# Hybrid decoder block on one core: the gates' first factors made once in the first chunk, kept in DRAM, and the head of the gates' stage reordered

## The chip, the cores and the metric

The kernel runs on one core of one Trainium2 chip. The metric is the device time in microseconds of that core. The core has a matrix engine (PE, with its weight loads shown as PEld), a vector engine (DVE), a scalar engine (ACT), a general engine (POOL), a queue engine (SP) and 16 DMA engines. SP issues nearly all DMAs; POOL issues those that add to their destination.

## What is computed

One decoder layer on x of 2048 tokens by 1024 channels, all in float32:

```python
h = rmsnorm(x, attn_norm)
z = h @ w_in                      # pool channels | q | k | v | gate_pool | gate_attn
g_pool, g_attn = split(sigmoid(z[..., o4:] + b_gate))
a = pool_mixer(u_pool, w_pool, pool_scale)     # windows 2, 4, 8, 16; per-group linear map
b = swa_sink_attention(q, k, v, sinks)         # window 128, QK-norm, partial rotary
x = x + (g_pool * a + g_attn * b) @ w_out
h = rmsnorm(x, ffn_norm)
up = causal_depthwise_conv(h @ w_up, conv_w, conv_b)
x = x + (silu(gate) * val) @ w_down
```

The change touches the gates: the two products of h with the 1024 gate columns each.

## The kernel before, in words

**Precision.** PE multiplies rounded float32 (`F32R`). Each operand is kept as a high part (ACT rounds it) and a low part (DVE takes the difference), and a product is three matmuls: high x high, high x low, low x high.

**Stages.** The sequence is cut into two chunks of 1024 tokens (`T`), so all stages run twice. In a chunk, `mixer` makes keys, values and queries, then attention, then calls `gates`; `out_proj`, `up` and `Down` follow. Attention is 32 items: four groups of four heads, in the order `q4` = 3, 2, 1, 0, each with eight blocks of 128 queries. Between two items stand matmuls that fill PE, the `fillers` of that group: projections of queries (`q`), pool channels (`pu`) and the gates of channel slabs 6 and 7 (`ga`, `pg`). In the last group (number 3) the last two items' fillers are the first products of the gates' stage, `one` and `two` of units 0 and 1.

**The gates' stage.** It computes the gates of the other six slabs, one `Gates` unit each (`u0` to `u5`). A unit multiplies a 2 x 2 block matrix (k halves by the two gates) with a 2 x 2 block input (k halves by token halves) in seven block products in place of eight: `one` to `seven`, and `early` for the product with `B22` where it is issued before its sum. So it needs sums of weight blocks and sums of input blocks, each split in high and low parts. The weight side is made by `Blocks` (line 326) from two raw slabs of 512 KB in four steps: `first` gives A11 and A12, `second` gives A22, `third` gives S3 and S2, `fourth` gives S1 and S4. A whole-size step is an ACT pass (L348) and a DVE pass (L349) over 128 x 1024, done by `halved`; `second` and the sums use half-size operations (L364 to L377). With `early` the last two steps change places. The input side is made from `xT`: `load_input` (L1386) loads a tile of 128 x 2 x 1024, `scale_input` (L1394) multiplies it by the norm's gain on ACT (L1397), and `right_t1` to `right_t4` (L1122 to L1154) make the sums T1 to T4 and split them by `parted` (L1032, L1033).

**What sets the order.** Weights come by a `Stream`: `get` hands out the next entry of `weight_order`, asks for raw tiles two entries ahead, and splits the next ones. A pair for the gates has the key `("gates", i)`. The order on each engine follows the program, but an instruction may be put earlier where its inputs and buffers are there and the engine is free; `issue_after` forbids it for single ones. Each engine then runs its own list strictly in order, and SP and POOL do so with their DMAs: one that waits holds all behind it. Buffers are pools of tagged slots: `U` has 19 (8 KB a partition), `R`, for raw weights, 3, `M` 5, `F` 4, `Q` 6. In PSUM the scores have one bank pair, `s`, which all exponentials of an item (L880) must have read before the next scores (L861).

**Kept weights.** The second chunk reads made weights back: `keep_weights` stores some, and for the two first pairs of the up-projection `Blocks.store` writes all four parts to DRAM tiles and `Kept.fetch` loads them by name (`PARTS`).

Of the kernel before, what the change touches and what calls it, by code (L numbers as in the profile page):

```python
# [16 lines left out]
F32 = mybir.dt.float32  # L17
F32R = mybir.dt.float32r
I32 = mybir.dt.int32
U8 = mybir.dt.uint8  # L20
AF = mybir.ActivationFunctionType
ALU = mybir.AluOpType
# [4 lines left out]
P = 128  # L27
# [112 lines left out]
def fillers(c, i):  # L140

    q = queries_of(0) + queries_of(1)
    g = gates_of(0)
    pu = [pooled_of(j) for j in range(4)]
    if i == 3:
        out = [[f] for f in g[6:] + pu[3]]
        out[3].insert(0, ("gates", 0, 0))
        out[5].insert(0, ("gates", 1, 0))
        return out + [[("one", i, 0), ("two", i, 0)] for i in range(2)]
    fold = [("fold", j, 0) for j in FOLDS[FOLD_FIRST:] if c == 0 and i == 0]  # L150
    out = fold + (q[:4] + pu[0][2:] + q[4:6], q[6:] + pu[1][:2] + g[:2] + pu[1][2:],
                  pu[2][:2] + g[2:6] + pu[2][2:])[i]
    return [out[n * len(out) // NB:(n + 1) * len(out) // NB] for n in range(NB)]


# [50 lines left out]
def block_kernel(ctx: ExitStack, tc: tile.TileContext, x, xT, pos, vec, qkn, w_poolT, w_pool, w_q, w_kv,  # L206
# [9 lines left out]
    up_ = pool("up", 19)  # L216
# [8 lines left out]
    def load(dst, src):  # L225
        nc.sync.dma_start(dst, src)

    def split(hi, lo, src):
        n = src.shape[1] // 2
        for i in range(2):  # L230
            t = slice(i * n, (i + 1) * n)
            high = A.copy(hi[:, t], src[:, t])  # L232
            low = V.tensor_sub(lo[:, t], src[:, t], hi[:, t].bitcast(F32))  # L233
        return high.ins, low.ins

    def halves(h, t, src, gain):

# [69 lines left out]
    class Kept:  # L307


        def __init__(self, f):  # L310
            self.f, self.w = f, {}
# [15 lines left out]
    class Blocks:  # L327
# [3 lines left out]

        def __init__(self, raws, early=False):
            self.raws, self.w, self.at = raws, {}, 0
            self.steps = [self.first, self.second] + [self.third, self.fourth][::-1 if early else 1]
            self.tiles = []

        def store(self, f):
            kept[f] = []  # L340
            for i, t in enumerate(self.tiles):
                kept[f].append(dp.tile(list(t.shape), F32, f"kept_{f}_{i}"))
                load(kept[f][-1], t.bitcast(F32))

        def halved(self, first, second, raw):
            t = up_.tile([P, 2, 8, P], F32R, "U")
            self.tiles.append(t)
            A.copy(t[:, 0], raw)  # L348
            V.tensor_sub(t[:, 1], raw, t[:, 0].bitcast(F32))  # L349
            self.w[first], self.w[second] = t[:, :, 0:4], t[:, :, 4:8]  # L350

        def step(self, n=1):
            for _ in range(n):
                if self.at < 4:
                    self.steps[self.at]()
                    self.at += 1

        def first(self):
# [65 lines left out]
    class Input:  # L424
# [8 lines left out]
        def pair(self, j, n):  # L433
            return self.t[j, n]

        def fresh(self, k):
            if k % 2 == 0:
                for n in range(2):
                    self.t[k // 2, n] = up_.tile([P, 2, 2, 512], F32R, "U")

    def make_h(c, n, hs, ks=range(KT)):

        a, b = ((0, 256), (256, 512), (512, T))[n] if c == 0 else (0, T)
        for k in ks:
            gain = vc[:, V_AN + k:V_AN + k + 1]
            if n == 0:
                hs.fresh(k)
            if c == 0:
                halves(hs.at(k, n // 2), slice(a % 512, a % 512 + b - a), xs0[k // 2][:, k % 2, a:b], gain)
            else:  # L450
                src = mp.tile([P, T], F32, "M")
                load(src, xT[k * P:(k + 1) * P, c * T:(c + 1) * T])
                for i in range(2):
                    halves(hs.at(k, i), slice(0, 512), src[:, 512 * i:512 * i + 512], gain)
# [562 lines left out]
    def filler(kind, j, n, *a):  # L1017
        if kind == "fold":
            fold(j)
        elif kind == "gates":  # L1020
            a[-1]["units"][j].w = stream.get("gates", j)
        elif kind in ("one", "two"):
            getattr(a[-1]["units"][j], kind)()
        else:
            {"ga": gate_attn, "pu": pooled, "pg": gated, "q": queries}[kind](a[0], j, n, *a[1:])
# [93 lines left out]
        normed(xg[j], 0, pb)  # L1119
        b.setdefault("B11" if j < 2 else "B21", []).append(parted(xg[j][:, :, N0]))  # L1120

    def right_t1(xg, b, pb):  # L1122
        for j in range(2):
            normed(xg[j], 1, pb)
            q11, q12 = xg[j][:, :, N0], xg[j][:, :, N1]
            V.tensor_sub(q11, q12, q11)
            b.setdefault("T1", []).append(parted(q11))
# [259 lines left out]
    def load_input(c, j):  # L1387

        t = up_.tile([P, 2, T], F32, "U")
        load(t, xT[2 * j * P:(2 * j + 2) * P, c * T:(c + 1) * T]  # L1390
             .rearrange("(k p) t -> p k t", p=P))
        return t
# [7 lines left out]
    def gates(c, units, b, xg, last_probabilities, last_values):  # L1400


        def weights(f, n):
            if f < len(units):
                if units[f].w is None:
                    units[f].w = stream.get("gates", f)
                units[f].w.step(n)

        u0, u1, u2 = units[:3]
        xg += [load_input(c, j) for j in (2, 3)]  # L1410
        weights(2, 1)
        u2.one("t")
        last_probabilities()
        weights(1, 2)
        u2.two()
        last_values()
        u0.four()
        u0.early()
        for j in (2, 3):
            scale_input(xg[j], j)  # L1420
        t2s = right_t2(xg, b, None)
        u1.four("a")
        u1.early()
        right_t3(xg, b)
        u0.three()
        u0.six()
        weights(1, 1)
        u0.five()
        right_t4(xg, b, t2s)
        u0.fetch()  # L1430
        u1.three()
        u1.six()
        u0.attn()
        u0.seven()
        u0.value()
        weights(2, 1)
        u1.five()
        u0.combine()
        weights(2, 2)
        n = len(units)  # L1440
        for f in range(2, n):
            u, old = units[f], units[f - 1]
            if f > 2:
                u.one()
                u.two()
            old.fetch()
            old.attn()
            weights(f + 1, 1)
            if f == n - 1:
                mixes = {j: mixed(j) for j in (3, 2, 1)}  # L1450
            old.seven()
            old.value()
            weights(f + 1, 1)
            u.three()
            u.four()
            old.combine()
            if f == n - 1:
                ms = {j: [parted(mixes[j][:, :, N0])] for j in (3, 2, 1)}
                x0 = up_.tile([P, 2, 2, 512], F32R, "U")
                old.parts(x0)  # L1460
                stream.part(stream.used + 2)
            weights(f + 1, 1)
            u.five()
            u.early()
            u.six()
            weights(f + 1, 1)
        u.fetch()
        u.attn()
        u.value(N1)
        u.seven()  # L1470
        u.value(N0)
        for c_ in (N0, N1):
            u.combine(c_)
            if c_ == N0:
                u.parts(x0)
        ms[0] = [x0]
        return ms, mixes
# [144 lines left out]
    def mixer(c, hs, kvw):  # L1622
# [49 lines left out]
        for i in range(len(items)):  # L1672
            group, n = divmod(i, NB)
            chain = scores(items[i])
            if i + 2 < len(items):
                load_queries(items[i + 2])
            if i > 1:
                values(items[i - 2])
            run_later(0)
            fills = fillers(c, group)[n]  # L1680
            last = chain
            for j, f in enumerate(fills):
                if i > 0 and j == (len(fills) > 1):
                    last = probabilities(items[i - 1], chain)
                if j == (len(fills) > 1):
                    run_later(2, last)
                filler(*f, c, hs, ta, st)
            if group == 3:
                if 3 <= n < 7:
                    units[0].w.step(1)  # L1690
                if n == 5:
                    run_later(9)
                    units[1].w.step(1)
                    xg.append(load_input(c, 0))
                if n == 6:
                    scale_input(xg[0], 0)
                    xg.append(load_input(c, 1))
                if n == 7:
                    scale_input(xg[1], 1)
        values(items[-2])  # L1700
        run_later(9)
        right_t1(xg, b, None)
        return gates(c, units, b, xg, lambda: probabilities(items[-1]), lambda: values(items[-1]))

    high, low = split_weights.last
# [103 lines left out]
```

## Time and profile before

| | us |
|---|---|
| median of 3 runs | 2420.15 (2419.64 to 2424.95) |
| the profiled run | 2421.1 |
| its span, first to last instruction | 2419.2 |
| groups 1 and 2 of attention, first chunk | about 195 to 315 |
| group 3, first chunk | about 315 to 376 |
| joint of attention and gates' stage, first chunk | 365 to 420 |
| the same joint, second chunk | 1557 to 1612 |

How to read the profile. The page gives the busy time of each engine, and its share of the span. The table by stage gives, for a stretch of time, the busy time of each engine with the number of instructions, the granted clock of PE (1.00 is full), the share in which the 16 DMA engines were busy, and the rate. A row of the timeline gives start, duration, engine, line, operation, the tile written and the tiles read, the shapes, how many instructions were merged, and in brackets how long the engine had been idle before and what it waited for. A row of the groups gives the busy time and mean ns, then the idle time before. A row of DMA issues ends with the number, the size of one and the median time from issue to landing.

### The profile page before, as it was taken

How to read it: one execution, taken by the hardware profiler on the slowest of the kernel's cores; microseconds unless marked ns; L12 is line 12 of the kernel's file. 1: busy time of each engine (PE TensorE's matmuls, PEld its weight loads, DVE VectorE, ACT ScalarE, POOL GpSimd, SP SyncE). 2: the span in 40 equal slices, each digit the busy share in tenths (PEclk: the TensorE clock that was granted, in tenths of full speed). 3: DMA queues.
4: the chain of work that ended last, by engine and by line, in shares of the span. 5: the costliest groups of instructions: out<-in, count | busy, mean ns of one | idle time of the engine just before them, and what ended most of it. 6: DMA issues, size and time to landing. Idle time of an engine off the chain costs nothing.

```text
span 2419.2 us, 30260 instructions
## 1 busy us (share of the span) xinstructions
PE 2376.2 (98%) x11108; PEld 1971.5 (81%) x11108; DVE 1906.2 (79%) x2934; ACT 1187.9 (49%) x2179; POOL 178.4 (7%) x118
## 2 busy tenths in 40 slices
PE   8999998999999999999999999999999999999999
PEld 7888886877888888788888888778888888888887
DVE  8678888876977777799946867898578777779994
ACT  6545446454555555543622544464546545454432
POOL 0114221000000000000002232200000000000000
PEclk9999999999999999999999999999999999999999
DMA  9568765688222333545244675546742222228421
GB/s 358 203 191 245 222 179 170 212 278 308 90 79 82 101 115 105 190 175 165 96 154 138 185 210 169 161 140 222 226 170 90 93 88 79 79 70 287 140 70 52
DMA packets 160404, 386.08 MB, mean 160 GB/s; under 512 B 13952, under 2 KB 50304, under 8 KB 152320
## 3 DMA queue, kind: packets, MB, share of 16 engines
q1 hardware_dynamic: 155472, 375.58, 46.5%
q0 software_dynamic: 4352, 8.39, 2.2%
q8 instruction: 87, 1.43, 0.2%
q14 instruction: 61, 0.50, 0.1%
q10 hardware_dynamic: 432, 0.19, 0.0%
HBM read 258.93 MB, written 125.17 MB: 159 GB/s over the span
## 4 chain that ended last, share of the span: by engine, by line
PE 88%; DVE 4%; DMA 3%; ACT 3%; issue 1%; POOL 0%; SPq 0%; DVEq 0%; ACTq 0%
PE f L1159 22%; PE f L249 22%; PE t L1159 13%; PE a L1159 6%; PE f L1603 4%; PE a L1603 4%; PE s L1603 4%; PE t L1603 4%; PE a L922 2%; PE s L861 2%; PE a L249 1%; PE t L894 1%; DMA U<-xT 1%; DMA tad<-U 1%; ACT Q L880 0%
## 5 line engine op out<-in xcount | busy, mean ns | idle before, releaser
L249 PE MATMUL f<-U,U 128*128 128x512 f32 (+1 forms) x2784 | 649.2, 389 | 7.5 <-ACT U L232 3.4
L249 PEld LDWEIGHTS f<-U,U 128*128 128x128 f32 x2784 | 510.2, 188 | 113.4 <-DVE U L233 4.9
L1159 PE MATMUL f<-U,U 128*128 128x512 f32 x1872 | 450.1, 391 | 4.5 <-ACT Q L1177 4.5
L1159 PEld LDWEIGHTS f<-U,U 128*128 128x128 f32 x1872 | 352.6, 189 | 80.0 <-ACT Q L1177 6.2
L1225 DVE SCALAR_TENSOR_TENSOR M<-F,vc,M 128x1024 f32<-128x1024 f32 x176 | 225.2, 1281 | 140.8 <-ACT M L1222 140.5
L1159 PE MATMUL t<-U,U 128*128 128x512 f32 x1392 | 330.0, 391 | 6.1 <-ACT U L348 3.6
L1159 PEld LDWEIGHTS t<-U,U 128*128 128x128 f32 x1392 | 262.0, 189 | 62.5 <-ACT U L348 4.4
L348 ACT CAST U<-R 128x1024 fp32r<-128x1024 f32 x156 | 163.1, 1053 | 72.3 <-DVE R L377 37.4
L349 DVE TENSOR_TENSOR U<-R,U 128x1024 fp32r<-128x1024 f32 x156 | 190.7, 1226 | 2.7 <-ACT U L348 2.7
L1159 PE MATMUL a<-U,U 128*128 128x512 f32 x768 | 187.3, 391 | 0.0
L1159 PEld LDWEIGHTS a<-U,U 128*128 128x128 f32 x768 | 143.5, 188 | 29.9 <-ACT Q L1177 0.4
L1159 PE MATMUL f<-U,M 128*128 128x512 f32 x624 | 150.7, 389 | 0.3 <-DVE F L1203 0.3
L880 ACT ACTIVATE Q<-s,st,rq 128x128 f32<-128x128 f32 x256 | 113.8, 456 | 53.1 <-DVE st L877 52.7
L1159 PEld LDWEIGHTS f<-U,M 128*128 128x128 f32 x624 | 117.1, 188 | 25.0 <-DVE F L1203 0.8
L902 POOL TENSOR_SCALAR_AFFINE_SELECT M<-M 128x1024 fp32r<-128x1024 f32 x64 | 97.4, 1522 | 372.5 <-DVE st L882 246.0
L1211 ACT COPY F<-f 128x512 f32<-128x512 f32 x52 | 30.5, 586 | 186.2 <-PE f L1159 186.2
L1561 ACT CAST U<-U 128x1024 fp32r<-128x1024 f32 x76 | 79.0, 1051 | 83.6 <-PE s L1603 21.6
L1222 ACT ACTIVATE M<-F,vc 128x1024 f32<-128x1024 f32 x88 | 109.4, 1243 | 2.0 <-DVE F L1207 0.5
L929 ACT COPY U<-a 128x512 f32<-128x512 f32 x64 | 37.6, 588 | 117.5 <-PE a L922 117.3
L1562 DVE TENSOR_TENSOR U<-U,U 128x1024 fp32r<-128x1024 f32 x76 | 91.9, 1218 | 3.3 <-ACT U L1561 3.1
L1561 ACT CAST F<-U 128x1024 fp32r<-128x1024 f32 x44 | 46.1, 1049 | 93.5 <-PE a L1603 63.8
L1177 ACT COPY Q<-f 128x512 f32<-128x512 f32 x104 | 60.8, 585 | 60.7 <-PE f L1159 60.6
(280 smaller groups left out, 3747.8 us busy)
## 6 DMA issues: line engine op xcount, KB each, us to landing
R<-w_up SPq DMA_DIRECT2D x80, 512.0 KB, 3.8
actd<-M SPq DMA_DIRECT2D x44, 512.0 KB, 2.7
U<-w_down SPq DMA_DIRECT2D x88, 256.0 KB, 5.2
U<-actd SPq DMA_DIRECT2D x88, 256.0 KB, 5.3
qd<-U SPq DMA_DIRECT2D x64, 256.0 KB, 3.8
Q<-qd SPq DMA_DIRECT2D x64, 256.0 KB, 4.7
R<-w_out SPq DMA_DIRECT2D x32, 512.0 KB, 5.2
U<-kept SPq DMA_DIRECT2D x12, 1024.0 KB, 6.7
```

The lines of the kernel that those rows point to most:

```text
L249: nc.tensor.matmul(out, a, b, start=(i == 0), stop=(i == n - 1))
L348: A.copy(t[:, 0], raw)
L349: V.tensor_sub(t[:, 1], raw, t[:, 0].bitcast(F32))
L880: A.activation(pr[:, h, :], sc[:, h, 0:P], AF.Exp, bias=nm[:, h:h + 1], scale=it["rq"][:, h:h + 1], accum_out=rs[:, h:h + 1])
L902: G.affine_select(own.rearrange("p a h q -> p (a h) q"), pa.bitcast(F32).rearrange("p a h q -> p (a h) q"), pattern=[[0, 8], [1, P]], base ...
L1159: nc.tensor.matmul(bank, a[:, x, k, :], b[k // 2][:, y, k % 2, :], start=(first and i == 0), stop=(i == 11), skip_group_check=True)
L1177: Up.last = A.copy(t, bank).ins
L1222: A.activation(y, u[:, 2:], AF.Identity, bias=cw[:, 3, m:m + 1], scale=cw[:, 2, m:m + 1])
L1225: V.scalar_tensor_tensor(y, u[:, j:j + T], cw[:, j, m:m + 1], y, op0=ALU.mult, op1=ALU.add)
L1561: A.copy(hi, src)
L1562: V.tensor_sub(lo, src, hi.bitcast(F32))
L1603: nc.tensor.matmul(into[m], u[:, 0, c_], v[:, 1], start=(first and j == 0), stop=(k == n - 1 and j == 2), skip_group_check=True)
```

## The change

The pairs `gates` 0 and 1 leave group 3. In the first chunk they are taken at the start of groups 1 and 2, and after every second item one step is made and stored to DRAM at once (`step(1)`, `store`). For these two pairs `halved` no longer subtracts on DVE: ACT writes the high part and the negated input, and a DMA from POOL adds the input to the latter (`split_added`). In both chunks group 3 and the gates' stage then fetch the parts by `Kept`. `Blocks` always makes its steps in the order 1, 2, 3, 4. The first step of unit 2 moves from the stage into group 3, the loads of `xT` tiles 0 and 1 and the first half of `right_t1` move one item or more forward, the loads of tiles 2 and 3 stand behind `last_values`, and the rest of the stage's head is reordered. At the start of the first chunk, a one-element memset on POOL takes the four input tiles of the second token half as soon as the others are taken.

```diff
 def fillers(c, i):
...
     if i == 3:
         out = [[f] for f in g[6:] + pu[3]]
-        out[3].insert(0, ("gates", 0, 0))
-        out[5].insert(0, ("gates", 1, 0))
         return out + [[("one", i, 0), ("two", i, 0)] for i in range(2)]
...
+    if c == 0 and i in (1, 2):
+        out = [[f] for f in out]
+        out[0].insert(0, ("gates", i - 1, 0))
+        return out
...
+    def split_added(hi, lo, src):
+
+        A.copy(hi, src)
+        A.activation(lo, src, AF.Copy, scale=-1.0)
+        G.dma_start(lo, src.bitcast(F32R), accum_op=ALU.add)
...
-        def __init__(self, raws, early=False):
-            self.raws, self.w, self.at = raws, {}, 0
-            self.steps = [self.first, self.second] + [self.third, self.fourth][::-1 if early else 1]
+        def __init__(self, raws, added=False):
+            self.raws, self.w, self.at, self.added = raws, {}, 0, added
             self.tiles = []
 
         def store(self, f):
-            kept[f] = []
-            for i, t in enumerate(self.tiles):
-                kept[f].append(dp.tile(list(t.shape), F32, f"kept_{f}_{i}"))
-                load(kept[f][-1], t.bitcast(F32))
+            done = kept.setdefault(f, [])
+            for i in range(len(done), len(self.tiles)):
+                t = self.tiles[i]
+                done.append(dp.tile(list(t.shape), F32, f"kept_{f}_{i}"))
+                load(done[-1], t.bitcast(F32))
 
         def halved(self, first, second, raw):
             t = up_.tile([P, 2, 8, P], F32R, "U")
             self.tiles.append(t)
-            A.copy(t[:, 0], raw)
-            V.tensor_sub(t[:, 1], raw, t[:, 0].bitcast(F32))
+            if self.added:
+                split_added(t[:, 0], t[:, 1], raw)
+            else:
+                A.copy(t[:, 0], raw)
+                V.tensor_sub(t[:, 1], raw, t[:, 0].bitcast(F32))
...
-        def fresh(self, k):
+        def fresh(self, k, first=False):
             if k % 2 == 0:
                 for n in range(2):
-                    self.t[k // 2, n] = up_.tile([P, 2, 2, 512], F32R, "U")
+                    t = self.t[k // 2, n] = up_.tile([P, 2, 2, 512], F32R, "U")
+                    if n == 1 and first:
+                        G.memset(t[:, 1, 1, 511:512].bitcast(F32), 0.0)
...
         elif kind == "gates":
-            a[-1]["units"][j].w = stream.get("gates", j)
+            a[-1]["early"] = stream.get("gates", j)
...
-    def right_t1(xg, b, pb):
-        for j in range(2):
+    def right_t1(xg, b, pb, js=range(2)):
+        for j in js:
...
         u0, u1, u2 = units[:3]
-        xg += [load_input(c, j) for j in (2, 3)]
-        weights(2, 1)
         u2.one("t")
         last_probabilities()
-        weights(1, 2)
+        right_t1(xg, b, None, (1,))
         u2.two()
         last_values()
+        xg += [load_input(c, j) for j in (2, 3)]
+        u0.w.fetch("S3", "S2")
+        u1.w.fetch("S3", "S2")
+        weights(2, 1)
         u0.four()
         u0.early()
         for j in (2, 3):
             scale_input(xg[j], j)
+        u0.w.fetch("A22")
         t2s = right_t2(xg, b, None)
         u1.four("a")
         u1.early()
         right_t3(xg, b)
         u0.three()
         u0.six()
-        weights(1, 1)
+        weights(2, 1)
         u0.five()
         right_t4(xg, b, t2s)
+        u1.w.fetch("A22")
         u0.fetch()
...
-        weights(2, 1)
         u1.five()
         u0.combine()
-        weights(2, 2)
+        weights(2, 1)
...
+            if c == 0 and group in (1, 2) and n % 2 == 1:
+                st["early"].step(1)
+                st["early"].store(f"gates{group - 1}")
             if group == 3:
-                if 3 <= n < 7:
-                    units[0].w.step(1)
+                if n == 3:
+                    units[0].w = Kept("gates0")
+                    units[0].w.fetch("A11", "A12")
+                if n == 4:
+                    units[1].w = Kept("gates1")
+                    units[1].w.fetch("A11", "A12")
+                    xg.append(load_input(c, 0))
                 if n == 5:
                     run_later(9)
-                    units[1].w.step(1)
-                    xg.append(load_input(c, 0))
+                    units[2].w = stream.get("gates", 2)
+                    units[2].w.step(1)
+                    xg.append(load_input(c, 1))
                 if n == 6:
+                    units[0].w.fetch("S1", "S4")
                     scale_input(xg[0], 0)
-                    xg.append(load_input(c, 1))
+                    right_t1(xg, b, None, (0,))
                 if n == 7:
+                    units[1].w.fetch("S1", "S4")
                     scale_input(xg[1], 1)
         values(items[-2])
         run_later(9)
-        right_t1(xg, b, None)
         return gates(c, units, b, xg, lambda: probabilities(items[-1]), lambda: values(items[-1]))
```

More of the change, by code (lines that the diff above doesn't have):

```diff
@@ L354, in step @@
                 if self.at < 4:
-                    self.steps[self.at]()
+                    (self.first, self.second, self.third, self.fourth)[self.at]()
                     self.at += 1
@@ L446, in make_h @@
             if n == 0:
-                hs.fresh(k)
+                hs.fresh(k, c == 0)
             if c == 0:
```

## The prediction

> **What bounds the kernel now.** I read the page first, then the view of waits for PE alone, then the timeline round the gates' stage, then the table by stage.
>
> ```profile
> span 2419.2 us, 30260 instructions
> PE 2376.2 (98%) x11108; PEld 1971.5 (81%) x11108; DVE 1906.2 (79%) x2934; ACT 1187.9 (49%) x2179; POOL 178.4 (7%) x118
> ```
> ```profile
> 0.00:80.00 80.00, 68.97 (x438) 60.81 (x439) 63.72 (x235) 55.18 (x128) 6.66 (x13) 0.98 0.86 313
> 195.00:255.00 60.00, 60.00 (x320) 51.14 (x319) 49.70 (x106) 34.80 (x103) 23.02 (x12) 1.00 0.82 234
> 255.00:315.00 60.00, 59.93 (x310) 50.58 (x309) 50.80 (x104) 28.66 (x97) 14.90 (x10) 1.00 0.69 196
> 365.00:420.00 55.00, 47.80 (x204) 37.50 (x203) 45.41 (x61) 34.63 (x64) 6.94 (x6) 0.94 0.60 179
> 1557.00:1612.00 55.00, 47.02 (x205) 37.26 (x204) 45.77 (x60) 33.72 (x55) 6.91 (x6) 0.94 0.59 177
> ```
>
> The columns of the second fence are the stretch, its length, the busy time of PE, PEld, DVE, ACT and POOL, the granted clock, the DMA share and GB/s. PE sets the time. The matmuls themselves are not changed, so only PE's idle time (43.0 us in the whole span) and a lowered clock can be won. Eleven microseconds of that idle time lie in the start-up, and the two joints between attention and the gates' stage hold 55 - 47.80 = 7.20 us and 55 - 47.02 = 7.98 us. Attention's groups 1 and 2 of the first chunk (195 to 315) have next to no PE idle time, and they are where the change puts new work. The timeline names each idle piece, first chunk and then second:
>
> ```profile
> 375.68 0.50 PE L922 MATMUL a<-M,U 128*128 128x512 f32 x1 [0.55 <-DVE M L899]
> 376.53 2.19 ACT L1397 ACTIVATE U<-U,vc 128x1024 f32<-128x1024 f32 x2 [3.73 <-DMA U<-xT]
> 380.52 1.22 PE L861 MATMUL s<-U,Q 128*128 128x256 f32 x8 [2.49 <-ACT Q L880]
> 390.84 0.73 PE L1159 MATMUL t<-U,U 128*128 128x512 f32 x2 [1.80 <-ACT U L348]
> 402.93 3.02 PE L1159 MATMUL t<-U,U 128*128 128x512 f32 x12 [0.68 <-ACT Q L1177]
> 416.80 4.84 PE L1159 MATMUL f<-U,U 128*128 128x512 f32 x20 [1.68 <-ACT Q L1177]
> ```
> ```profile
> 1566.50 0.49 PE L922 MATMUL a<-M,U 128*128 128x512 f32 x1 [0.29 <-DVE M L899]
> 1567.66 0.73 PE L922 MATMUL a<-M,U 128*128 128x512 f32 x2 [0.67 <-POOL M L902]
> 1568.52 1.15 ACT L1397 ACTIVATE U<-U,vc 128x1024 f32<-128x1024 f32 x1 [4.61 <-DMA U<-xT]
> 1571.47 2.08 PE L861 MATMUL s<-U,Q 128*128 128x256 f32 x8 [3.08 <-ACT Q L880]
> 1583.59 0.73 PE L1159 MATMUL t<-U,U 128*128 128x512 f32 x2 [1.77 <-ACT U L348]
> 1594.06 3.02 PE L1159 MATMUL t<-U,U 128*128 128x512 f32 x12 [0.68 <-ACT Q L1177]
> 1607.72 4.85 PE L1159 MATMUL f<-U,U 128*128 128x512 f32 x20 [1.50 <-ACT Q L1177]
> ```
> ```profile
> 381.00:386.00 5.00, 5.00 (x22) 4.12 (x21) 4.94 (x8) 4.06 (x7) 0.00 (x0) 0.66 0.98 399
> 391.00:396.00 5.00, 5.00 (x18) 3.95 (x19) 4.00 (x4) 3.39 (x4) 1.20 (x1) 0.66 0.02 3
> 1569.00:1577.00 8.00, 5.53 (x18) 4.76 (x19) 5.04 (x8) 7.53 (x16) 0.00 (x0) 0.57 0.90 331
> ```
>
> The biggest piece is a queue's doing: ACT sits 3.73 us before `scale_input` (L1397) because the input tile from `xT` has not landed, and attention's exponentials (L880), which stand behind it on ACT, free the score bank that PE waits for. The next (1.80, 1.77) is the first factor of `u2` (L348), made too late. The third (1.68, 1.50) is the copy (L1177) behind other work on ACT. After the idle pieces the granted clock falls: (1 - 0.66) x 5 = 1.7 us lost twice in the first chunk; in the second (1 - 0.57) x 8 = 3.4 us, of which about 0.9 us fell on time that was idle anyway, so 2.5. The two joints hold 7.2 + 3.4 and 8.0 + 2.5, together 21.1 us.
>
> **The change, part by part.** *What leaves the joint.* For each of `u0` and `u1` the four steps of `Blocks` go from both chunks' joints. Their prices:
>
> ```profile
> L348 ACT CAST U<-R 128x1024 fp32r<-128x1024 f32 x156 | 163.1, 1053 | 72.3 <-DVE R L377 37.4
> L349 DVE TENSOR_TENSOR U<-R,U 128x1024 fp32r<-128x1024 f32 x156 | 190.7, 1226 | 2.7 <-ACT U L348 2.7
> ```
> ```profile
> L365 DVE TENSOR_TENSOR M<-R,M 128x512 fp32r<-128x512 f32 x2 | 1.4, 686 | 1.7 <-ACT M L364 1.7
> L364 ACT CAST M<-R 128x512 fp32r<-128x512 f32 x2 | 1.2, 618 | 0.0
> ```
>
> One unit is 3 x 1.23 + 5 x 0.69 = 7.1 us of DVE and 3 x 1.05 + 0.62 = 3.8 us of ACT. Two units relieve the joint of 14.2 and 7.5 us, where DVE is busy 45.4 of 55 us; `u2`'s first step moves ahead one item into that room. `right_t1` is only split and moved earlier (per tile 1.2 + 1.05 + 1.2 us). *What comes in.* Eight loads from `kept` replace four raw loads, and `xT` tiles 0 and 1 are asked for one item (7.8 us) earlier:
>
> ```profile
> U<-kept SPq DMA_DIRECT2D x12, 1024.0 KB, 6.7
> U<-xT SPq DMA_DIRECT2D x8, 1024.0 KB, 9.7
> R<-wfold SPq DMA_DIRECT2D x8, 512.0 KB, 7.1
> tad<-U POOLq DMA_DIRECT2D x16, 512.0 KB, 8.5
> ```
>
> ACT waited 3.73 and 4.61 us for `xT`; 7.8 us cover both if the loads do go out earlier. I count the 2.49 and 3.08 as 0.3 afterwards (won 2.2 and 2.8), the 0.55 and 0.29 + 0.67 as gone with DVE's load, the 1.80 and 1.77 as gone because `u2`'s first factor is made two items ahead. The 0.68 stays: `u0.early` still follows `u0.four` into the same bank and waits for its copy. The 1.68 and 1.50 fall only to 1.0, since `u0.five` needs a copy in the same way: 0.7 and 0.5. Sum: 5.2 us and 6.0 us. Of the clock I take three quarters, 2.6 and 1.9, as gaps near 1 us remain. The joints give 7.8 + 7.9 = 15.7 us; the bounds are 0 and 21.1 less four copies of 0.68, 18.4.
>
> By the Trainium skill's page "TensorE: Matmul & The Clock Gate", section "Why this matters for your kernels", gaps up to some 3 us keep the clock, so the gaps of 2.49 and 1.80 us should not have lowered it. The trace shows it at 0.66 behind both, so the measurement decides; going by the page, the first chunk's 2.6 us would not come back, and the sum would be 13.1.
>
> *What groups 1 and 2 of the first chunk take on.* `split_added` replaces three L349 per unit by three more ACT passes (3 x 1.05 us) and three accumulating DMAs from POOL (each some 1 us of POOL's queue, with the affine selects of attention behind it). With the five half-size operations left, DVE gains 3.4 us in groups where it is busy 49.7 and 50.8 of 60 us; ACT gains 6.9 us at 34.8 and 28.7. PE's work covers both. The stores wait on SP for the accumulate, and the loads of queries are queued behind them. The DMA engines are the tight resource:
>
> ```profile
> 306.50:311.00 4.50, 4.50 (x23) 3.73 (x22) 3.53 (x10) 4.04 (x14) 1.49 (x1) 1.00 0.89 115
> 255.00:260.00 5.00, 5.00 (x28) 4.28 (x27) 2.59 (x7) 1.08 (x7) 1.04 (x1) 1.00 1.01 371
> ```
>
> In the first stretch an accumulate into `tad` runs nearly alone: 0.89 x 4.5 = 4.0 us of all engines for 512 KB. Plain transfers reach 371 GB/s. A unit adds 3 x 4.0, 3.67 MB of stores (9.9 us) and 1.05 MB of raw loads (2.8 us): 24.7 us. Beside the 0.82 x 60 = 49 and 0.69 x 60 = 41 us now, that is 74 and 66 us of demand in 60 us. If all overflow stopped PE, it would cost 20 us; at the other end nothing, as much can wait. I take 3.5 us, near the lower end, because weights are loaded far ahead of use (next fence: pair 0's last slab at 254.14, its matmuls from 322.88). The memsets that take four input tiles early (start-up, PE idle 11 us there) I cost at 0, between -2 and +2: POOL is busy 6.66 of 80 us, but four buffers are held sooner.
>
> The sum: -15.7 + 3.5 = -12.2 us. The profiled run took 2421.1 us (1.9 outside its span of 2419.2), 1 us above the median of 2420.15; from the median that gives **2408.0 us**.
>
> **Rivals.**
>
> ```profile
> 254.14 0.50 SPq L226 DMA_DIRECT2D R<-w_gp  x1
> 322.88 1.40 PE L249 MATMUL f<-U,U 128*128 128x512 f32 x5
> ```
> ```profile
> 364.78 1.99 DVE L349 TENSOR_TENSOR U<-R,U 128x1024 fp32r<-128x1024 f32 x1 [0.18 <-ACT U L348]
> 366.80 0.34 SPq L226 DMA_DIRECT2D R<-w_gp  x1
> 367.23 0.39 SPq L226 DMA_DIRECT2D U<-xT  x1
> ```
> ```profile
> 253.04 5.72 PE L249 MATMUL f<-U,U 128*128 128x512 f32 x24
> 260.80 1.40 PE L249 MATMUL f<-U,U 128*128 128x512 f32 x5
> ```
>
> *Raw buffers run out (slower).* There are three `R` buffers, and a gates pair holds two from load until its steps are through: at 366.80 a raw load goes out just when such a step (L349, ends 366.77) has freed one. In the change this happens throughout groups 1 and 2. If the fourth step of `u0` runs where it is written, behind the matmul at 253.04, its operations and two ACT passes beside exponentials end near 259, the accumulate lands 1 + 8.5 us later, only then `pu` slab 2 can be loaded (7.1 us) and its first half split (1.4 us): 277 to 280 with crowded queues, where PE wants it at 260.8. That is 16 to 20 us, plus 1.7 to 3.4 us of clock: 2420.15 - 12.2 + 19 = 2427, at most 2431. It decides against the change from a stall of 17 us. Against it: steps are issued as soon as buffers allow, and the loads run far ahead. With the 3.2 us that the Trainium skill's page "DMA: Bandwidth & Descriptors", section "Anatomy of one DMA", gives for such an accumulate by its fit (an estimate; the trace's 8.5 goes to DRAM), the stall would be 5 us shorter and the time 2422.
>
> *The late tiles move the stall (no change).* `xT` tiles 2 and 3 are now asked for behind `last_values`. If they go out some 10 us later, `T2` and `T3` come late and `u0.three` waits some 4.5 us and loses 1 us of clock, in both chunks: 2408 + 11 = 2419.
>
> *`xT` 0 and 1 are no earlier (no change).* The load at 367.23 stood on SP behind a raw load that waited for its buffer. If such a place in SP's order keeps it late, the 2.2 and 2.8 us and their clock (1.7 + 1.9) stay lost: 2408 + 8.6 = 2417.
>
> **How the numbers follow.** Forecast 0.60 (2402 to 2414); raw buffers 0.15; late tiles 0.13; `xT` no earlier 0.12. A measurement of this kernel tells about 0.2% (4.8 us) from no change. Faster than 2415.3: 0.59 of the forecast and 0.02 of the last rivals, 0.61. Slower than 2425: most of the raw buffers and a crowd of transfers worse than taken, 0.16. Within: 0.23. The range runs from 2400, where the joints give their bound of 18.4 and groups 1 and 2 lose nothing, to 2424, and leaves out the worse half of the first rival.
>
> **What would show it.** Right: at both joints PE no longer waits behind L880 and L348, no idle on ACT before L1397, clock 1.00; groups 1 and 2 with PE busy above 58 of 60 us. Wrong: PE idle near the first matmuls of group 2, released by a split weight (L232, L233) or by L880 after a late query load; or PE waiting at `u0.three` for L1032 and L1033.

## The result: 0.2% slower, with the second chunk's joint as forecast and the first chunk's attention not

| | us |
|---|---|
| kernel before, median | 2420.27 (2417.43 to 2425.86) |
| changed kernel, median | 2426.21 (range at full clock 2421.72 to 2430.28) |
| ratio, with its 95% interval | 1.0019 (1.0011 to 1.0027) |
| predicted | 2408.0 (2400 to 2424) |

The change makes the kernel a little slower, where the prediction had it 0.5% faster. Two of the changed kernel's 17 runs went at a lower clock (2624.34 and 3967.15 us); the range and the ratio leave them out, and the median of the other 15 is 2425.47 us, from which differences to the changed kernel are taken below. The profile of the changed kernel read here is that of a further run (2425.69 us). Lines of the old file from 250 on stand some 8 to 13 lines further down: L880 is L893, L348 is L359, L232 is L234. The page first:

```profile
span 2424.0 us, 30326 instructions
...
PE 2378.2 (98%) x11108; PEld 1971.4 (81%) x11108; DVE 1882.0 (78%) x2912; ACT 1187.4 (49%) x2177; POOL 181.5 (7%) x128
```

PE has the same matmuls and is idle 45.8 us in place of 43.0: what was won in one place was lost in another. The table by stage of the changed kernel shows where. The columns are those of the prediction's second fence. The joints stand some 9 to 15 us later than before, so their stretches are moved.

```profile
0.00:80.00 80.00, 73.67 (x470) 65.22 (x471) 65.03 (x238) 55.74 (x130) 7.24 (x17) 1.00 0.92 335
195.00:255.00 60.00, 55.51 (x283) 46.16 (x282) 43.04 (x92) 32.78 (x92) 23.98 (x14) 0.97 0.85 252
255.00:315.00 60.00, 54.72 (x270) 44.81 (x269) 48.73 (x97) 31.39 (x92) 14.45 (x10) 0.97 0.96 307
315.00:380.00 65.00, 61.01 (x300) 51.20 (x299) 47.08 (x101) 34.15 (x102) 14.27 (x11) 0.95 0.89 281
380.00:435.00 55.00, 47.66 (x211) 38.24 (x210) 39.27 (x55) 28.68 (x52) 6.21 (x5) 0.94 0.70 212
1566.00:1621.00 55.00, 53.05 (x244) 42.70 (x245) 42.47 (x62) 31.34 (x60) 7.28 (x6) 1.00 0.76 224
```

The start-up is better (PE 73.67 of 80 us, 68.97 before). The second chunk's joint is better (53.05 of 55 at clock 1.00, 47.02 at 0.94). The first chunk's joint is no better (47.66 of 55, 47.80 before). Groups 1 and 2 of the first chunk, where PE had no idle time, now have 4.5 + 5.3 us of it and a clock of 0.97. From 195 to 435 PE is idle 60 - 55.51 + 60 - 54.72 + 65 - 61.01 + 55 - 47.66 = 21.1 us, and the clock takes 0.03 x 120 + 0.05 x 65 + 0.06 x 55 = 10.2 us more: 31 us, against 7.3 + 3.3 before (the same stages, 195 to 365 at full clock and then the joint to 420).

The same by marks that move with the work (own sums from the two traces: the start of the first exponential, L880 or L893, of attention's items 0, 8, 16, 24 and 30 of a chunk, and of the first sum of the output projection, L1079 before):

| stage | before, us | changed: difference |
|---|---|---|
| start to item 0 | 139.4 | -7.4 |
| group 0, first chunk | 61.4 | +0.2 |
| group 1 | 60.8 | +12.0 |
| group 2 | 62.2 | +2.9 |
| group 3 up to item 30 | 54.8 | +7.5 |
| item 30 to the output projection | 128.7 | -1.6 |
| from there to item 24, second chunk | 1007.0 | -0.7 |
| second chunk, items 24 to 30 | 55.3 | -4.2 |
| second chunk, item 30 to the output projection | 128.7 | -3.4 |
| rest | 720.9 | -0.4 |

They add up to +4.8 us, the difference of the two spans (2424.0 and 2419.2).

**Groups 1 to 3.** The waits of DVE and ACT for DMAs from 195 to 345 us, first all of the kernel before, then the largest of the changed one with a wait of PE behind DVE, and SP's own (us in all, times, longest):

```profile
DVE R L368 <- DMA R<-w_gp: 1.1, 1, 1.1
ACT Q L880 <- DMA Q<-qd: 0.3, 1, 0.3
```
```profile
DVE R L379 <- DMA R<-w_gp: 8.5, 2, 5.9
...
PE t L907 <- DVE Q L899: 7.5, 5, 4.0
ACT U L234 <- DMA R<-wfold: 7.3, 2, 5.1
```
```profile
SPq L228 <- DMA U<-R: 36.7, 6, 9.4
```

Raw weights come late. ACT stands before the split of a slab (L234) and DVE before a sum of raw blocks (L379), and attention's exponentials and quotients (L899) are queued behind them. The last row is SP's: it stood 36.7 us before DMAs (stores of the parts, and raw loads) that needed the end of one of the six accumulates `U<-R`. The timeline of the changed kernel, one engine at a time, shows one such chain:

```profile
246.68 0.87 POOL L242 DMA_DIRECT2D U<-R  x1 [5.33 <-ACT U L241]
```
```profile
256.81 0.32 SPq L228 DMA_DIRECT2D R<-wfold  x1
```
```profile
261.79 1.14 ACT L234 CAST U<-R 128x512 fp32r<-128x512 f32 x2 [5.09 <-DMA R<-wfold]
```
```profile
262.44 1.29 DVE L235 TENSOR_TENSOR U<-R,U 128x512 fp32r<-128x512 f32 x2 [4.64 <-ACT U L234]
```

The accumulate issued at 246.68 landed at 256.74 by the trace. It reads the raw slab, so the slab's `R` buffer was held until then, and 0.07 us later the next raw slab went out. By the trace SP's own record shows it standing from 248.46 to 256.76 before this load, until that accumulate's semaphore came. The slab landed at 261.77, and ACT had waited 5.09 us for it. A subtract on DVE would have freed the buffer when it ended.

Not every wait is of this kind. One piece of PE ended with a load of queries that went out in time, at 247.24, and landed at 260.18, 12.9 us later, where the median of such loads in this stretch is 6.7 us:

```profile
260.31 1.08 PE L876 MATMUL s<-U,Q 128*128 128x128 f32 x8 [1.63 <-DMA Q<-qd]
```

That load was late on its way, not for want of a buffer. And before PE's wait of 4.00 us in group 3 (first row under the joints below) SP stood from 321.54 to 330.87 before a store of a made part, which waited for the last accumulate; the raw load that DVE lacked stood behind this store, and its buffer, by the order of the loads, was held by the same accumulate. There the trace alone does not tell the queue from the buffer; the experiments do.

How much the DMA engines carried is told by the rows of groups 1 and 2, cut at the marks above, first of the changed kernel, then of the one before:

```profile
193.60:266.40 72.80, 66.69 (x330) 55.19 (x329) 49.61 (x109) 38.13 (x109) 25.82 (x15) 0.95 0.88 265
266.40:331.40 65.00, 61.34 (x313) 50.81 (x312) 55.76 (x115) 38.24 (x109) 17.82 (x13) 1.00 0.94 291
```
```profile
200.80:261.60 60.80, 60.80 (x324) 51.79 (x323) 47.95 (x105) 32.81 (x103) 24.07 (x12) 1.00 0.90 268
261.60:323.80 62.20, 62.13 (x320) 52.43 (x319) 52.71 (x110) 30.71 (x102) 14.94 (x10) 1.00 0.70 206
```

They were busy 0.88 x 72.8 + 0.94 x 65.0 = 125 us, against 0.90 x 60.8 + 0.70 x 62.2 = 98 before.

**The joints.** PE's larger idle pieces in the changed kernel, in group 3 and the joint of the first chunk, and then at the second chunk's joint:

```profile
342.20 1.09 PE L907 MATMUL t<-identr,Q 128*128 128x128 f32 x4 [4.00 <-DVE Q L899]
393.91 0.80 PE L935 MATMUL a<-M,U 128*128 128x512 f32 x1 [4.64 <-ACT M L909]
430.26 4.17 PE L1172 MATMUL f<-U,U 128*128 128x512 f32 x17 [1.68 <-ACT Q L1190]
```
```profile
1566.27 0.63 PE L907 MATMUL t<-identr,Q 128*128 128x128 f32 x4 [0.94 <-DVE Q L899]
1597.16 0.73 PE L935 MATMUL a<-M,U 128*128 128x512 f32 x2 [0.98 <-POOL M L915]
```

In neither joint does PE wait for the exponentials or for `u2`'s first factor any more: the 2.49, 3.08, 1.80 and 1.77 us are gone. But the first chunk has a new piece of 4.64 us, released by the copy of the probabilities (L909). ACT's timeline there:

```profile
383.87 1.06 ACT L1045 CAST U<-U 128x1024 fp32r<-128x1024 f32 x1
392.32 1.04 ACT L1045 CAST U<-U 128x1024 fp32r<-128x1024 f32 x1 [7.39 <-issue]
393.27 0.58 ACT L909 CAST M<-t 128x512 fp32r<-128x512 f32 x1
```

The second half of the early `right_t1` splits its sum at 392.32 (L1045, `parted`). The sum was ready at 382.5 by the trace, yet ACT stood 7.39 us before it, with the probabilities behind it. By the trace ACT's own record at L1045 stands from 383.40 to 392.28 before two semaphores. One had been complete since 380.61; the other is that of POOL's accumulate into `tad`, issued at 381.29, whose last update came at 392.26. So the split waited for that accumulate to land. The accumulate reads a `U` buffer and the split writes one, and they share nothing else, so what the split lacked is taken to be this buffer.

### The profile page after: what moved, and what is told of

The parts are those of the page before. It is cut to its first block, busy times and chain, and to the rows that moved or that the text cites. A ratio compares the mean times of both kernels' runs of the same rounds, so it can differ in the third digit from the quotient of the medians.

```text
span 2622.6 us, 30326 instructions
## 1 busy us (share of the span) xinstructions
PE 2597.0 (99%) x11108; PEld 2025.5 (77%) x11108; DVE 1893.2 (72%) x2912; ACT 1193.2 (45%) x2177; POOL 182.6 (7%) x128
## 4 chain that ended last, share of the span: by engine, by line
PE 91%; DMA 4%; DVE 3%; ACT 1%; issue 1%; POOL 0%; SPq 0%; DVEq 0%; ACTq 0%; POOLq 0%
PE f L1172 24%; PE f L257 23%; PE t L1172 13%; PE a L1172 7%; PE a L1619 4%; PE f L1619 4%; PE s L1619 4%; PE t L1619 4%; PE a L935 2%; PE s L874 2%; PE a L257 1%; PE t L907 1%; DMA tad<-U 1%; DMA R<-w_gp 1%; DMA R<-wfold 1%
## 5 line engine op out<-in xcount | busy, mean ns | idle before, releaser
L257 PE MATMUL f<-U,U 128*128 128x512 f32 (+1 forms) x2784 | 715.9, 416 | 4.4 <-DVE U L235 2.1
L257 PEld LDWEIGHTS f<-U,U 128*128 128x128 f32 x2784 | 525.8, 194 | 156.2 <-DVE U L235 5.0
L1172 PE MATMUL f<-U,U 128*128 128x512 f32 x1872 | 491.9, 417 | 1.5 <-ACT Q L1190 1.4
L1172 PEld LDWEIGHTS f<-U,U 128*128 128x128 f32 x1872 | 359.9, 192 | 111.9 <-ACT Q L1190 3.1
L1172 PE MATMUL t<-U,U 128*128 128x512 f32 x1392 | 362.6, 417 | 0.0
L1172 PEld LDWEIGHTS t<-U,U 128*128 128x128 f32 x1392 | 267.6, 192 | 81.4
L1172 PE MATMUL a<-U,U 128*128 128x512 f32 x768 | 205.0, 418 | 0.0
L359 ACT CAST U<-R 128x1024 fp32r<-128x1024 f32 x144 | 150.5, 1050 | 96.8 <-DVE R L388 36.1
L360 DVE TENSOR_TENSOR U<-R,U 128x1024 fp32r<-128x1024 f32 x144 | 175.5, 1221 | 5.3 <-ACT U L359 5.3
L1172 PE MATMUL f<-U,M 128*128 128x512 f32 x624 | 165.8, 417 | 0.0
L1172 PEld LDWEIGHTS f<-U,M 128*128 128x128 f32 x624 | 119.8, 192 | 36.7 <-DVE F L1216 0.3
L893 ACT ACTIVATE Q<-s,st,rq 128x128 f32<-128x128 f32 x256 | 113.8, 456 | 58.2 <-DVE st L890 54.2
```

The source lines that it names most:

```text
L257: nc.tensor.matmul(out, a, b, start=(i == 0), stop=(i == n - 1))
L893: A.activation(pr[:, h, :], sc[:, h, 0:P], AF.Exp, bias=nm[:, h:h + 1], scale=it["rq"][:, h:h + 1], accum_out=rs[:, h:h + 1])
L1172: nc.tensor.matmul(bank, a[:, x, k, :], b[k // 2][:, y, k % 2, :], start=(first and i == 0), stop=(i == 11), skip_group_check=True)
```

## The experiments

Each ratio, with its 95% interval, is to runs of the kernel before on the same chip, whose median was 2420.3 to 2422.0 us. Differences between two changed kernels are of medians, partly from different chips; taken from the ratios they come out up to 2 us otherwise, and where it matters both are given.

**The changed kernel again** (2425.69 us; the profile above).

> The changed kernel as it is, for a profile at the clock of the kernel before. All theories: some 2425 us; the two joints between attention and the gates' stage have under 3 us of PE idle time each (7.2 and 8.0 before), and PE's idle time in attention's groups 1 and 2 of the first chunk (0.07 us before) is what eats the gain: 15 to 25 us with the lowered clock. They differ in what ends those waits: queue theory, SP stands behind stores that wait for the accumulates of POOL, and raw weights and queries go out late; traffic theory, the DMAs go out in time and land late; raw-buffer theory, raw loads wait for a free R buffer.

**The second chunk alone.** The first chunk makes its factors as before, in group 3 and the stage, and stores them; the second chunk is as changed. There is no memset.

```diff
+            if group == 3 and c == 0:
+                if 3 <= n < 7:
+                    units[0].w.step(1)
+                    units[0].w.store("gates0")
...
+            elif group == 3:
                 if n == 3:
                     units[0].w = Kept("gates0")
```

> The first chunk is as in the kernel before (steps in group 3 and in the stage, DVE subtracts), plus stores of the factors as they are made; the second chunk fetches them and has the new order. All theories: the second chunk's joint alone, 8 us less PE idle time and clock, minus 0 to 4 us for 7 MB of stores: 2412 to 2416 us. If the time is near 2420, the gain at the joint is given back behind it and the loss is not in groups 1 and 2 alone.

Measured 2419.00 us, 0.9992 (0.9983 to 1.0001). By the marks the second chunk won 4.3 + 3.1 us, as in the changed kernel, and the start-up and groups 0 to 2 of the first chunk were within 0.5 us of before. But the stores came at a price of their own: in this kernel's timeline, PE and then ACT at the first chunk's joint,

```profile
389.84 0.79 PE L934 MATMUL a<-M,U 128*128 128x512 f32 x1 [5.46 <-ACT M L908]
```
```profile
385.67 2.19 ACT L1409 ACTIVATE U<-U,vc 128x1024 f32<-128x1024 f32 x2 [3.44 <-DMA U<-xT]
```

ACT waits for `xT` as before, and the joint loses where it was to be left alone (-4.7 to item 30, +10.2 after it). That the stores delay `xT` on SP is argued, not tried. The loss of groups 1 and 2 is in the first chunk's new work, but this kernel doesn't give the second chunk's gain by itself: 2412 to 2416 us were expected.

**DVE subtracts again.** Everything else stays as changed.

```diff
-            return Blocks(raws, key[0] == "gates" and key[1] < 2)
+            return Blocks(raws)
```

> The changed kernel with the low parts of the first two pairs made by DVE's subtraction again, no accumulating DMA. Queue theory: the stores no longer wait for an accumulate, the idle time of groups 1 and 2 goes: 2410 to 2416 us. Traffic theory: 12 of 24.7 us of added DMA time per group go, half of the loss: 2415 to 2420 us. Raw-buffer theory: the pairs still hold two of three buffers for a whole group: 2422 to 2427 us.

Measured 2414.04 us, 0.9965 (0.9951 to 0.9978): the accumulates cost 11.4 us of the changed kernel's time (13.1 by the ratios). Three rows of its table by stage, from the shortest of its four runs (2410.07 us):

```profile
195.00:255.00 60.00, 57.14 (x298) 47.73 (x296) 46.78 (x98) 32.50 (x97) 23.46 (x12) 1.00 0.85 265
255.00:315.00 60.00, 56.74 (x290) 46.99 (x291) 56.30 (x111) 32.86 (x96) 15.29 (x9) 1.00 0.91 289
315.00:365.00 50.00, 50.00 (x258) 42.32 (x257) 41.54 (x88) 26.45 (x81) 10.10 (x8) 1.00 0.91 305
```

The clock is full again, PE is busy 57.14 and 56.74 us where it was 55.51 and 54.72, and up to the joint it has no idle time in group 3. All this with three DVE passes more per unit. By the ranges set before the run this is the queue theory's result, and the raw-buffer theory's (2422 to 2427) failed: it left out that a DVE pass frees a buffer sooner than an accumulate does. The next two kernels tell the two apart.

**The stores one item later,** behind that item's load of queries, to see whether SP's standing before them does the harm.

```diff
...
+                elif n > 0:
+                    with tc.issue_after(last_query):
+                        st["early"].store(f"gates{group - 1}")
...
```

> The changed kernel with each part's store issued one item later, behind that item's query load on SP; same transfers, same accumulates. Queue theory: SP no longer stands before the stores, 2410 to 2418 us. Traffic and raw-buffer theory: no change, 2422 to 2428 us.

Measured 2427.35 us, 1.0028 (1.0019 to 1.0038). SP's row of the waits, which read 36.7 us, is now

```profile
SPq L228 <- DMA U<-R: 19.1, 4, 6.8
```

Half of SP's standing is gone and nothing is won. This speaks against the queue behind the stores as the main cost; the 19.1 us that are left were not taken away here.

**The raw slabs of pairs 0 and 1 elsewhere,** both in one `U` buffer; the accumulates stay.

```diff
+        if kind == "gates" and a[0] < 2:
+            both_ = up_.tile([P, 2, 8, P], F32, "U")
+            for i, src in enumerate(srcs):
+                load(both_[:, i], src)
+            return [both_[:, 0], both_[:, 1]]
```

> The changed kernel, accumulates as they are, but the raw slabs of the first two gates pairs lie in one U buffer and leave the three R buffers to the other weights. Raw-buffer theory (the accumulates keep the raw slabs till they land, so later raw loads go out late and ACT and DVE stand before them): 2412 to 2418 us, and neither ACT nor DVE waits for R loads in groups 1 and 2. Traffic theory (the added transfers themselves): no change, 2423 to 2428 us. In between, 2418 to 2423: both.

Measured 2414.94 us (2413.34 to 2421.53), 0.9978 (0.9968 to 0.9989): 10.5 us come back with the accumulates in place (9.9 by the ratios). So the `R` buffers are short; how much of that is the accumulates' doing, the kernel with both edits tells. Its trace is of the longest of its ten runs, 2421.53 us, so it shows little of this gain, but it shows what stays. SP stands nearly as long as in the changed kernel, and ACT waits for a raw slab whose load went out at 244.72 and landed 13.9 us later:

```profile
SPq L228 <- DMA U<-U: 34.5, 6, 9.1
```
```profile
258.65 1.14 ACT L234 CAST U<-R 128x512 fp32r<-128x512 f32 x2 [7.08 <-issue]
```

With SP's standing left as it was, the kernel is shorter by about 10 us: the queue is not the main cost. And one DVE wait for a raw slab (5.4 us) is left too, where none was expected.

**The traffic of the accumulates alone:** DVE subtracts, and six accumulates of the same size go from POOL into a scratch tile in DRAM; no instruction waits for them.

```diff
...
+                        G.dma_start(scratch, hs.pair(0, 0)[:, 0].bitcast(F32), accum_op=ALU.add)
...
```

> Low parts by DVE (as in the run at 2414 us), and beside each of these steps an accumulating DMA of 512 KB from POOL whose data nobody uses: an input tile added to a scratch tensor in DRAM. Nothing but scratch waits for it. Traffic theory: the loss comes back, 2422 to 2428 us. Raw-buffer theory: nothing is held by it, 2412 to 2417 us.

Measured 2419.57 us (2413.5 to 2421.9), 0.9993 (0.9984 to 1.0002): 5.5 us over the same kernel without them (6.8 by the ratios), a rough number by the spread of its runs. Neither expected range, 2422 to 2428 for traffic alone and 2412 to 2417 for buffers alone, holds it: the cost is in both. The groups of DMA issues in the changed kernel, and then in this one, 195 to 345 us:

```profile
U<-R POOLq DMA_DIRECT2D x6, 512.0 KB, 7.1
```
```profile
scratch<-U POOLq DMA_DIRECT2D x6, 512.0 KB, 9.3
```

They take 7.1 and 9.3 us to land. The scratch is in DRAM and the factors are not, so the two transfers are not quite alike.

**Both: DVE subtracts, and the raw slabs elsewhere.** The two edits above together.

> Both: low parts by DVE and the raw slabs of the pairs in a U buffer. Raw-buffer theory: the rest of the idle time in groups 1 and 2 (6 us of PE in the run with DVE's subtraction) shrinks, 2406 to 2412 us. Traffic theory: as with DVE's subtraction alone, 2412 to 2416 us.

Measured 2409.32 us, 0.9953 (0.9939 to 0.9966), 16.2 us below the changed kernel. The two edits form a square: 11.4 then 4.7 us, or 10.5 then 5.6 (by the ratios 13.1 then 2.9, or 9.9 then 6.1). Once the `R` buffers are free, the accumulates cost 5.6 us, which agrees with the 5.5 us of their traffic. The other 11.4 - 5.6 = 5.8 us (7.0 by the ratios) they cost only where `R` buffers are short, as a held buffer would. Whether the shortage costs anything with DVE's subtract, the 4.7 or 2.9 us, is not clear: the intervals of the two kernels overlap, and their profiled runs took 2410.07 and 2410.00 us.

**The same, with `right_t1` back behind the last item.**

```diff
-        right_t1(xg, b, None, (1,))
...
-                    right_t1(xg, b, None, (0,))
...
         run_later(9)
+        right_t1(xg, b, None)
```

> As the run before it, with both halves of T1 made behind the last item again, where the kernel before makes them. If the early T1 split stands on ACT before the last probabilities (a wait of 5.2 us on ACT in the first chunk's joint of the run with DVE's subtraction), PE's gap of 2.4 us there goes: 2 to 4 us faster than the run before it. If the late T1 delays the fourth product instead, 1 to 4 us slower.

Measured **2402.01 us** (2401.42 to 2405.98), 0.9927 (0.9915 to 0.9940): it beats both kernels, by 18.3 and 23.5 us. Its first chunk's joint, moved like the stretch above, and PE's largest piece in it:

```profile
358.00:413.00 55.00, 54.06 (x253) 43.78 (x252) 45.97 (x68) 34.57 (x64) 7.28 (x6) 1.00 0.79 242
```
```profile
390.46 0.74 PE L940 MATMUL a<-M,U 128*128 128x512 f32 x2 [0.40 <-POOL M L920]
```

**`right_t1` back, alone,** on the changed kernel.

> The changed kernel (2426.2 us) with one edit undone: both halves of right_t1 stand behind the last item again, as before the change. Theory A: the early place of T1 is a loss by itself (it puts ACT's splits ahead of the last items' probabilities in the first chunk's group 3); then the time falls by about what the same edit won on the kernel with DVE's subtract and the raw slabs elsewhere (2409.3 to 2402.0, 7.3 us): 2419, 2416 to 2421, and the gap of 4.65 us on the first chunk's joint is gone. Theory B: the late raw loads of the accumulating splits set the end of group 3 anyway; then the stall of T1 only lies beside it, and the time stays within 2 us of 2426.

Measured 2420.28 us, 0.9990 (0.9981 to 0.9999): 5.2 us won (7.0 by the ratios), so the early T1 costs by itself, whether or not the raw loads are late. PE's largest piece in the joint is 0.46 us, and its row:

```profile
373.00:428.00 55.00, 53.72 (x252) 43.48 (x251) 45.71 (x70) 34.97 (x66) 8.30 (x7) 1.00 0.77 242
```

**The memset alone,** on the kernel before.

```diff
...
-                    self.t[k // 2, n] = up_.tile([P, 2, 2, 512], F32R, "U")
+                    t = self.t[k // 2, n] = up_.tile([P, 2, 2, 512], F32R, "U")
+                    if n == 1 and first:
+                        G.memset(t[:, 1, 1, 511:512].bitcast(F32), 0.0)
...
```

> The kernel before (2420.3 us) with one edit of the change alone: the early memset that takes the four input tiles of the second token half at the start of the first chunk. Theory A: the 7.4 us by which the start-up is shorter in all runs that have the memset come from it and stay to the end: 2413, 2411 to 2415, and PE is busy over 73 of the first 80 us in place of 68.97. Theory B: the start-up is shorter but the time is given back later in the first chunk, or it comes from other edits: within 2 us of 2420.

Measured 2412.46 us, 0.9960 (0.9947 to 0.9972), so 9.7 us by the ratio (6.8 to 12.8). By the marks 6.9 us come in the start-up, and 2.6 in items 24 to 30 of the second chunk, which are not explained here. The waits of PE from 0 to 80 us, in the kernel before:

```profile
PE a L249 <- ACT U L238: 2.6, 4, 1.3
PE t L761 <- DVE U L763: 1.9, 1, 1.9
```

Both rows are gone with the memset. L238 is ACT's part of splitting the input (`halves`), eight passes for the second token half. The first two of them in the kernel before, and the first six in the kernel with the memset:

```profile
65.25 1.34 ACT L238 ACTIVATE U<-U,vc 128x512 fp32r<-128x512 f32 x2 [0.38 <-PE f L249]
```
```profile
35.51 0.73 ACT L238 ACTIVATE U<-U,vc 128x512 fp32r<-128x512 f32 x1
...
42.13 0.71 ACT L238 ACTIVATE U<-U,vc 128x512 fp32r<-128x512 f32 x1
...
43.60 2.57 ACT L238 ACTIVATE U<-U,vc 128x512 fp32r<-128x512 f32 x4
```

With its buffers taken at the start, the second token half is split from 35 us on, most of it by 46 us, while PE has other work. Before, its splits came only at 65 us, released by a matmul on PE, when PE was about to wait for them. The memset is the only edit and writes one element a partition of each tile, so it is the early hold of the buffers that moves the splits.

## Why the prediction was wrong, point by point

- **The second chunk's joint, 7.9 us: right.** The marks give 4.2 + 3.4 = 7.6 us. The waits behind the exponentials and behind `u2`'s factor are gone and the clock is 1.00, as the prediction asked. That the idle time left there, 1.95 us, is just what it kept is in part luck: both waits for the copy (0.68 and 1.50, of which it kept 0.68 and 1.0) are gone, and smaller pieces behind POOL and DVE came in their place.
- **The first chunk's joint, 7.8 us: the step "`right_t1` is only split and moved earlier" failed.** It counted the work of T1's splits and not what they wait for. In the changed kernel ACT stands before one of them with the probabilities behind it (4.64 us of PE, then half clock). With T1 back and the two other edits, the marks of the joint give 6.9 + 3.9 = 10.8 us, more than predicted. So the early `xT` loads and the earlier factors do what was said, and early T1 cost 5.2 to 7.3 us (both runs with it taken back).
- **Groups 1 and 2, 3.5 us: mis-sized, and the decisive step.** They cost 14.9 us by the marks, and the wait of 4.00 us in group 3 is theirs too (DVE's 5.9 us before `w_gp`, L379). The prediction priced the DMA engines' demand, 2 x 24.7 us, and took the low end "because weights are loaded far ahead of use". They are, but only as long as one of three `R` buffers is free. And the demand was too high: over the two groups the engines were busy some 27 us more, and not 49. It named the right mechanism as a rival, "raw buffers run out", with a chance of 0.15, and argued it away. What differs from that rival is the form: not one stall of 16 to 20 us near 260 to 280, but several of 1 to 4 us on PE, the larger ones with a stretch of lower clock. The prediction's sign of being wrong came in part: PE waited 1.63 us for a late load of queries near the start of group 2, and 2.11 us in group 1, which the view puts down to a split weight (L234), though a late load of queries landed 0.13 us before that wait ended.
- **Traffic.** Some 5.6 of the accumulates' 11.4 us are their traffic, and 5.8 go with the short buffers. With both edits groups 1 and 2 still take 3.7 + 3.6 us more than before by the marks, twice the 3.5 us that the prediction took for all of it; where these go was not tried.
- **The memset, 0 (-2 to +2): wrong by sign and size,** 7.4 us in the start-up. The prediction saw POOL's cost and the risk of buffers held, and not that a buffer taken early moves the work that fills it.
- **The rivals with late tiles and `xT` no earlier:** neither shows in the second chunk, and the first chunk's stage behind item 30 won 1.6 us. SP's order did make `xT` late in the kernel with only the second chunk changed.

From the predicted 2408.0: the memset -7.4, groups 1 to 3 and the joint of the first chunk +20.8 by the marks in place of -7.8 + 3.5, so +25.1, the second chunk +0.3, the other stages -0.9: 2425.1, beside the 2425.69 of the profiled run.

## What to carry to other kernels

A DMA in place of an engine's pass holds its source until it lands: where few buffers feed a stream of weights, price the hold (7.1 us in the median here and up to 10.1; a subtract is 1.2), not only the bytes. Work that is moved ahead stands on its engine ahead of what was there, so list what it waits for, its output buffer too. A gain in one chunk and a loss in the other can cancel to 0.2%: test the parts of such a change one by one. Here the memset wins, the kept factors and the new head of the stage win together at the joints, and the accumulates and the early T1 lose.

## What the hardware showed that I had not expected

The granted clock fell in steps after rather short waits. In the changed kernel's table by stage, round the waits of 4.00 and 4.64 us:

```profile
338.00:345.00 7.00, 3.00 (x10) 2.44 (x10) 5.60 (x11) 1.65 (x3) 0.00 (x0) 0.69 0.72 283
391.00:397.00 6.00, 2.87 (x8) 2.11 (x9) 3.08 (x6) 3.88 (x12) 1.09 (x1) 0.57 0.51 179
```

By the trace's clock records, both are stretches of 6.83 us at half clock, and the smaller idle pieces near 232 and 260 us (2.11 and 1.63 us) have 3.41 us each. At half clock 3.41 us lose 1.7 us, so these stalls of about 2 us cost about twice their length; the piece of 1.68 us near 430 and those under 1 us in the joints kept the full clock. By the Trainium skill's page "TensorE: Matmul & The Clock Gate", section "Why this matters for your kernels", gaps up to some 3 us keep the clock; these two did not, and neither did the 2.49 and 1.80 us in the kernel before, so the measurement decides. And plain engine work was cheaper than expected: with three DVE passes per unit back and the accumulates gone, DVE was busy 56.30 of 60 us from 255 to 315, and PE still lost less than in the changed kernel (56.74 us busy, 54.72 there).
